# Seven instead of six feature tiles accumulated during the input's norm, with the tokens loaded first

## The chip, the cores and the metric

One Trainium2 chip, one core. The metric is the device time of one execution in microseconds; several executions are timed and their median is given. The engines are TensorE (PE), VectorE (DVE), ScalarE (ACT), GpSimdE (POOL) and SyncE (SP, whose queue issues nearly all DMAs).

## What is computed

One layer of a hybrid diffusion backbone in float32: 512 latent tokens (x) and 256 context tokens (ctx) of width 1024. Every token is normalised and modulated by scale and shift that come from a vector; one wide projection feeds a convolution module, a bidirectional mLSTM and two gates per channel; then come the output projection and an MLP. Cut to what matters here:

```python
sh1_l, sc1_l, ga1_l, sh2_l, sc2_l, ga2_l = silu(c) @ w_mod + b_mod      # split in six
sh1_c, sc1_c, *_ = silu(c_ctx) @ w_mod + b_mod
hl = rmsnorm(x, norm1_g) * (1 + sc1_l) + sh1_l
hc = rmsnorm(ctx, norm1_g) * (1 + sc1_c) + sh1_c
pl = split(hl @ w_in); pc = split(hc @ w_in)
y_conv = silu(layernorm(dwconv31(pl[0] * sigmoid(pl[1])))) @ w_conv_out
h_c, states = bi_mlstm(pc); h_l = bi_mlstm(pl, states)
y_m = (rmsnorm(h_l) * sigmoid(pl[5])) @ w_m_out
y = sigmoid(pl[7]) * y_conv + sigmoid(pl[8]) * y_m
x += ga1_l * (y @ w_out);  x += ga2_l * (relu(modulate(rmsnorm(x))@w1)**2 @ w2)
out = rmsnorm(x, final_g)
```

`pl[7]` and `pl[8]`, the gates per channel, are 16 feature tiles of 128 channels. They need nothing but `hl`, and the change is about where some of them are computed.

## The kernel before

**Products.** Every product is done in three passes on PE (`mm3`, L101): each operand is split into a rounded part (`hi`, a cast on ACT) and the rest (`lo`, a subtraction on DVE), and hi·hi, hi·lo and lo·hi are summed in PSUM. A weight tile is loaded by `wpiece` (L88): DMA into `wraw` (three buffers), cast `whi` on ACT (four buffers), `wlo` on DVE (four). The scheduler places every engine's instructions in one fixed order when the program is built; each engine then goes through its list in that order.

**The start.** SP issues `col` (all small constants), the row `c`, one tile of modulation weights `wm`, the four token tiles `xt2` to `xt5`, the second `wm`, and then the weights `was`. `crow` (L160) spreads the row over 128 partitions by a matmul with ones (`pcr`) and applies SiLU, which gives `cL` (and later `cC` from `c_ctx`). `xnorm` (L179) handles a token tile of 128x1024: square with sum on ACT (L181), the reciprocal root on POOL in two small steps (`rstd_`, L76 to L78), then the tile is scaled on DVE (L183). `moddot` (L195) gives scale and shift of 128 features, `m1`: two products with a sum on DVE (L199) and three operations on one column. `hmake` (L206) transposes 128 features of the four token tiles on PE into a PSUM bank `pt`, applies scale and shift on ACT (`hf`, two buffers, shared with `so` below), casts `hT` on ACT (L107) and takes its low part on DVE (L108).

**The first loop.** It runs over the eight slices j of 128 input features. Each round loads a slice of the gates' weights (`was[j]`, 128 x NS·128), makes `hT[j]`, and adds its product to NS accumulators `sacc`, one bank each, so that PE has work while the norm of the next slice is made. PSUM has eight banks, in two pools of four, "a" and "b". With NS = 6 the accumulators hold all of "a" and two of "b"; `pt`, `pcr`, `pg` (the convolution's projection), `ptc` (the context's transposes) and `pab` (gates' tiles computed later) all come from "b".

**Behind it.** The context tokens are normalised, `cC` is made, and each accumulator goes through a sigmoid (`so`) to DRAM (`sd`). Then the convolution's tiles (`pg`, `up`, and 31 taps `ca` on DVE), the gate tiles `ab_early` (NX = 3 here and NE = 3 later), the queries and keys, with the context's slices (`ctxpart`) in between, and the gates of the mLSTM (`p`, with `zm` as the result of `finish`).

Of the kernel before, what the change touches and what calls it, by code (L numbers as in the profile page):

```python
# [8 lines left out]
F32 = mybir.dt.float32  # L9
# [4 lines left out]
P = 128  # L14
# [7 lines left out]
HD = 512  # L22
FF = 4096
NFF = FF // P
NS = 6
NX = 3
NE = 3
NWM = 4
LOWP = 800 
# [18 lines left out]
def block(ctx, tc, a, out):  # L48
# [8 lines left out]


    col = cst.tile([P, NCOL], F32, name="col")
    nc.sync.dma_start(out=col, in_=a["col"])  # L60
    ident = cst.tile([P, P], F32, name="ident")
    make_identity(nc, ident)
    ones = cst.tile([P, P], F32, name="ones")
# [9 lines left out]
    def ccol(o, n=1):  # L73
        return col[:, o:o + n]
# [68 lines left out]
    with ExitStack() as hs:  # L143
# [16 lines left out]
        def crow(src, nm):  # L160
            r_ = p0.tile([P, D], F32, name=nm)
            nc.sync.dma_start(out=r_[0:1, :], in_=src)
            for n in range(2):
                nn = slice(n * 512, (n + 1) * 512)
                pc = bank("pcr")
                mm(pc, lhsT=ones[0:1, :], rhs=r_[0:1, nn], start=True, stop=True)
                nc.scalar.activation(out=r_[:, nn], in_=pc, func=AF.Silu)
            return r_
        cL = crow(a["c"][0:1, :], "cL")
        ssq = p0.tile([P, 6], F32, name="ssq")  # L170
        rs = p0.tile([P, 6], F32, name="rs")

        def xload(t):
            xt = p0.tile([P, D], F32, name=f"xt{t}")
            src = a["ctx"][t * P:(t + 1) * P, :] if t < 2 else a["x"][(t - 2) * P:(t - 1) * P, :]
            nc.sync.dma_start(out=xt, in_=src)
            return xt

        def xnorm(t, xt):  # L179
            junk = p0.tile([P, D], F32, tag="jnk", name="junk")  # L180
            nc.scalar.activation(out=junk, in_=xt, func=AF.Square, scale=1.0 / 32.0, accum_out=ssq[:, t:t + 1])  # L181
            rstd_(rs[:, t:t + 1], ssq[:, t:t + 1], 1)
            nc.vector.tensor_scalar(out=xt, in0=xt, scalar1=rs[:, t:t + 1], scalar2=None, op0=ALU.mult)  # L183

        m1 = p0.tile([P, 2, KT, 2], F32, name="m1")

        def modload(j, parts=(1, 0)):
            r = {}
            for s in parts:
                raw = p0.tile([P, D], F32, tag="wm", name="wm", bufs=NWM)  # L190
                nc.sync.dma_start(out=raw, in_=a["wmt"][s, j])
                r[s] = raw
            return r

        def moddot(j, c, cv, raws=None):  # L195
            raws = raws or modload(j)
            for s in (1, 0):
                raw = raws[s]
                nc.vector.scalar_tensor_tensor(out=raw, in0=raw, scalar=1.0, in1=cv, op0=ALU.mult, op1=ALU.mult,  # L199
                                               accum_out=m1[:, c, j, s:s + 1])  # L200
                nc.vector.tensor_scalar(out=m1[:, c, j, s:s + 1], in0=m1[:, c, j, s:s + 1],
                                        scalar1=ccol(O_BM + s * KT + j), scalar2=None, op0=ALU.add)
            nc.vector.tensor_scalar(out=m1[:, c, j, 1:2], in0=m1[:, c, j, 1:2], scalar1=1.0,
                                    scalar2=ccol(O_G1 + j), op0=ALU.add, op1=ALU.mult)

        def hmake(j, c, pt, tl, o):  # L206
            n = len(tl) * P
            for i, xt in enumerate(tl):
                nc.tensor.transpose(pt[:, i * P:(i + 1) * P], xt[:, j * P:(j + 1) * P], ident)
            hf = p0b.tile([P, T], F32, tag="hf", name="hf")  # L210
            nc.scalar.activation(out=hf[:, :n], in_=pt[:, :n], func=AF.Identity, scale=m1[:, c, j, 1:2],
                                 bias=m1[:, c, j, 0:1])
            split(hT[j][:, 0, o:o + n], hT[j][:, 1, o:o + n], hf[:, :n])

        raw0 = modload(0, (1,))
        xl = [xload(t + 2) for t in range(NT)]
        raw0 |= modload(0, (0,))
        for t in range(NT):
            xnorm(t + 2, xl[t])
        sacc = [(bank_a if i < 4 else bank)("sacc") for i in range(NS)]  # L220
        for j in range(KT):
            w = wpiece(a["was"][j], (NS, P))
            moddot(j, 0, cL, raw0 if j == 0 else None)
            hmake(j, 0, bank("pt"), xl, C)
            for i in range(NS):
                mm3(sacc[i], (w[0][:, i, :], w[1][:, i, :]), hsl(j, C, T), j == 0, j == KT - 1)
        xc = [xload(t) for t in range(2)]
        for t in range(2):
            xnorm(t, xc[t])
        cC = crow(a["cc"][0:1, :], "cC")  # L230
        for i in range(NS):
            so = p0b.tile([P, T], F32, tag="hf", name="so")
# [730 lines left out]
def build(shapes):  # L963
    import concourse.bacc as bacc
    import concourse.tile as tile

    nc = bacc.Bacc("TRN2", target_bir_lowering=False, num_devices=1)
    aps = {k: nc.dram_tensor(f"in_{k}", s, F32, kind="ExternalInput").ap() for k, s in shapes.items()}
    out = nc.dram_tensor("out_0_dram", (T, D), F32, kind="ExternalOutput").ap()
    with tile.TileContext(nc) as tc:  # L970
        block(tc, aps, out)
    return nc
# [10 lines left out]
```

## Time and profile before

| | |
|---|---|
| median of three timed runs | 1370.1 us (1367.97 to 1663.36) |
| the profiled execution | 1365.75 us, span 1364.0 us |
| PE, DVE, ACT, POOL busy | 97%, 70%, 44%, 4% of the span |
| mean granted TensorE clock | 0.993 |
| memory traffic over the span | 128 GB/s |

A row of the trace reads: start in us from the span's start, duration, engine, line, operation, output <- inputs, and in brackets how long the engine had stood idle and what ended that. Names are given without buffer numbers. A row "waited for" sums those idle times by the one that ended them.

### The profile page before, as it was taken

The page shows a single profiled execution, that of the slowest core. Times are in us where ns is not written, and L with a number is a line of the kernel's source. Part 1 is how long each engine was busy: PE and PEld are TensorE (multiplying, and loading weights), DVE is VectorE, ACT ScalarE, POOL GpSimd, SP SyncE. Part 2 cuts the span into 40 slices and gives each one's busy share as a digit, 9 for nine tenths or more (in the row PEclk, how much of TensorE's full clock was granted, in tenths as well). Part 3 has the DMA queues.
Part 4 walks back from the last instruction along what each step waited for, and adds up shares of the span by engine and source line. Part 5 has one row for each costly group of instructions (what it writes and reads, how often), then busy time and mean ns, then how long its engine had stood idle before and what let it go on. Part 6 is the DMA issues. An engine that isn't in the chain of part 4 may idle for free.

```text
span 1364.0 us, 16728 instructions
## 1 busy us (share of the span) xinstructions
PE 1327.2 (97%) x6264; PEld 1104.6 (81%) x6264; DVE 949.7 (70%) x1508; ACT 606.3 (44%) x931; POOL 55.3 (4%) x199
## 2 busy tenths in 40 slices
PE   5999899999999999999999999998999999999997
PEld 4788788888888888888888887787788888888886
DVE  6799988489674995849995464677676454545554
ACT  5547554446534465334645363222465322442232
POOL 1000100000000000000000000000010000000001
PEclk9999999999999999999999999999999999999999
DMA  8883233123322223221334465777623322333211
GB/s 316 291 318 99 87 97 120 62 67 97 108 93 63 77 88 120 79 76 64 108 93 145 153 232 185 253 260 225 204 77 115 102 78 77 123 109 94 69 54 62
DMA packets 64885, 175.30 MB, mean 129 GB/s; under 512 B 6546, under 2 KB 18978, under 8 KB 64804
## 3 DMA queue, kind: packets, MB, share of 16 engines
q1 hardware_dynamic: 64804, 174.23, 39.3%
q8 instruction: 49, 0.80, 0.2%
q14 instruction: 32, 0.26, 0.1%
HBM read 161.94 MB, written 12.26 MB: 128 GB/s over the span
## 4 chain that ended last, share of the span: by engine, by line
PE 79%; DMA 8%; DVE 6%; ACT 3%; issue 2%; POOL 1%; SPq 0%; ACTq 0%; POOLq 0%; DVEq 0%
PE pf L104 8%; PE pf L103 8%; PE pf L102 8%; PE pv L102 3%; PE pv L104 3%; PE pv L103 3%; DMA wraw<-in_wmo 2%; PE pl L102 2%; PE pg L104 2%; PE pg L102 2%; PE pl L103 2%; PE pq L104 2%; PE pq L102 2%; PE pq L103 2%; PE pl L104 2%
## 5 line engine op out<-in xcount | busy, mean ns | idle before, releaser
L97 ACT CAST whi<-wraw 128x1024 fp32r<-128x1024 f32 (+1 forms) x159 | 165.1, 1040 | 318.7 <-PE pv L104 74.6
L98 DVE TENSOR_TENSOR wlo<-wraw,whi 128x1024 fp32r<-128x1024 f32 (+1 forms) x159 | 191.6, 1207 | 97.7 <-ACT whi L97 96.9
L376 DVE SCALAR_TENSOR_TENSOR ca<-up,col,ca 128x512 f32<-128x512 f32 x240 | 179.6, 749 | 5.5 <-ACT ca L374 0.9
L336 DVE SCALAR_TENSOR_TENSOR cacc<-craw,col,cacc 128x512 f32<-128x512 f32 (+1 forms) x128 | 110.7, 880 | 0.1
L102 PE MATMUL pf<-w2h,fT 128*128 128x512 f32 x256 | 99.6, 389 | 0.0
L103 PE MATMUL pf<-w2l,fT 128*128 128x512 f32 x256 | 99.6, 389 | 0.0
L104 PE MATMUL pf<-w2h,fT 128*128 128x512 f32 x256 | 99.6, 389 | 0.0
L857 ACT CAST w2h<-w2raw 128x1024 fp32r<-128x1024 f32 x32 | 32.2, 1051 | 133.7 <-PE pf L104 107.1
L102 PE MATMUL pf<-h2T,whi 128*128 128x512 f32 x224 | 87.1, 389 | 0.0
L103 PE MATMUL pf<-h2T,whi 128*128 128x512 f32 x224 | 87.1, 389 | 0.0
L104 PE MATMUL pf<-h2T,wlo 128*128 128x512 f32 x224 | 87.1, 389 | 0.0
L877 DVE TENSOR_TENSOR x<-pf,x 128x512 f32<-128x512 f32 x64 | 44.1, 689 | 61.7 <-PE pf L104 61.7
L102 PE MATMUL pv<-whi,hT 128*128 128x512 f32 x192 | 75.4, 393 | 0.0
L104 PE MATMUL pv<-whi,hT 128*128 128x512 f32 x192 | 74.7, 389 | 0.0
L103 PE MATMUL pv<-wlo,hT 128*128 128x512 f32 x192 | 74.7, 389 | 0.0
L855 DVE TENSOR_TENSOR w2raw<-w2raw,ga 128x1024 f32<-128x1024 f32 x32 | 39.0, 1225 | 48.7 <-DMA w2raw<-in_w 47.7
L103 PEld LDWEIGHTS pf<-w2l,fT 128*128 128x128 f32 x256 | 48.1, 188 | 10.0
L102 PEld LDWEIGHTS pf<-w2h,fT 128*128 128x128 f32 x256 | 48.1, 188 | 10.0
L104 PEld LDWEIGHTS pf<-w2h,fT 128*128 128x128 f32 x256 | 48.1, 188 | 9.9
L103 PE MATMUL p<-wlo,hT 128*128 128x512 f32 x128 | 50.6, 395 | 2.4 <-DVE wlo L98 2.4
L102 PE MATMUL p<-whi,hT 128*128 128x512 f32 x128 | 50.8, 397 | 1.3 <-DVE zm L309 1.3
L645 DVE SCALAR_TENSOR_TENSOR wmt<-wmt,cB 128x1024 f32<-128x1024 f32 x32 | 39.1, 1223 | 17.5 <-DMA wmt<-in_wmt 15.6
(351 smaller groups left out, 3353.9 us busy)
## 6 DMA issues: line engine op xcount, KB each, us to landing
wm<-in_wmt SPq DMA_DIRECT2D x32, 512.0 KB, 5.7
wraw<-in_wqk SPq DMA_DIRECT2D x32, 512.0 KB, 3.5
wmt<-in_wmt SPq DMA_DIRECT2D x32, 512.0 KB, 3.8
wraw<-in_w SPq DMA_DIRECT2D x32, 512.0 KB, 3.6
w2raw<-in_w SPq DMA_DIRECT2D x32, 512.0 KB, 3.6
wraw<-in_wglu SPq DMA_DIRECT2D x16, 512.0 KB, 3.9
wraw<-in_wp SPq DMA_DIRECT2D x16, 512.0 KB, 3.6
wraw<-in_wv SPq DMA_DIRECT2D x16, 512.0 KB, 3.6
```

The source lines that it names most:

```text
L97: nc.scalar.copy(out=hi[:, s], in_=raw[:, s])
L98: nc.vector.tensor_tensor(out=lo[:, s], in0=raw[:, s], in1=hi[:, s].bitcast(F32), op=ALU.subtract)
L102: mm(dst, lhsT=l[0], rhs=r[0], start=start, stop=False)
L103: mm(dst, lhsT=l[0], rhs=r[1], start=False, stop=False)
L104: mm(dst, lhsT=l[1], rhs=r[0], start=False, stop=stop)
L336: nc.vector.scalar_tensor_tensor(out=acc[:, :n], in0=raw[:, d:d + n], scalar=ccol(wc + d), in1=acc[:, :n], op0=ALU.mult, op1=ALU.add)
L376: nc.vector.scalar_tensor_tensor(out=accv, in0=up[:, :, d:d + 64], scalar=w_, in1=accv, op0=ALU.mult, op1=ALU.add)
L645: nc.vector.scalar_tensor_tensor(out=raw, in0=raw, scalar=1.0, in1=cB, op0=ALU.mult, op1=ALU.mult, accum_out=modc[:, ch, j:j + 1])
L855: nc.vector.tensor_tensor(out=raw, in0=raw, in1=ga2, op=ALU.mult)
L857: nc.scalar.copy(out=hi, in_=raw)
L877: nc.vector.tensor_tensor(out=x1[t][:, nn], in0=pf, in1=x1[t][:, nn], op=ALU.add)
```

## The change

Seven accumulators instead of six (NS), two early gate tiles instead of three (NX), so the number of matmuls is unchanged and `was` pieces grow from 128x768 to 128x896. The four token tiles are loaded ahead of `col` and of both first `wm` tiles. The squares of the second and the fourth token tile are done on DVE with a sum, the others stay on ACT. The scale of a token tile is done in two pieces, columns 0 to 255 first and the other 768 behind the first `hmake`. `b1`, the modulation's offset plus one, is made once on POOL, so `moddot` has two small operations instead of three. The scratch for dynamic DMA is set to 4096.

```diff
-NS = 6
-NX = 3
+NS = 7
+NX = 2
@@
     col = cst.tile([P, NCOL], F32, name="col")
-    nc.sync.dma_start(out=col, in_=a["col"])
@@
-        def xnorm(t, xt):
-            junk = p0.tile([P, D], F32, tag="jnk", name="junk")
-            nc.scalar.activation(out=junk, in_=xt, func=AF.Square, scale=1.0 / 32.0, accum_out=ssq[:, t:t + 1])
+        cL = crow(a["c"][0:1, :], "cL")
+        xl = [xload(t + 2) for t in range(NT)]
+        nc.sync.dma_start(out=col, in_=a["col"])
...
+        def xstat(t, xt, dve=False):
+            junk = p0.tile([P, D], F32, tag=f"jnk{int(dve)}", name="junk")
+            if dve:
+                nc.vector.scalar_tensor_tensor(out=junk, in0=xt, scalar=1.0 / D, in1=xt, op0=ALU.mult, op1=ALU.mult,
+                                               accum_out=ssq[:, t:t + 1])
+            else:
+                nc.scalar.activation(out=junk, in_=xt, func=AF.Square, scale=1.0 / 32.0, accum_out=ssq[:, t:t + 1])
             rstd_(rs[:, t:t + 1], ssq[:, t:t + 1], 1)
-            nc.vector.tensor_scalar(out=xt, in0=xt, scalar1=rs[:, t:t + 1], scalar2=None, op0=ALU.mult)
+
+        def xscale(t, xt, o, n):
+            nc.vector.tensor_scalar(out=xt[:, o:n], in0=xt[:, o:n], scalar1=rs[:, t:t + 1], scalar2=None, op0=ALU.mult)
@@ moddot
-                nc.vector.tensor_scalar(out=m1[:, c, j, s:s + 1], in0=m1[:, c, j, s:s + 1],
-                                        scalar1=ccol(O_BM + s * KT + j), scalar2=None, op0=ALU.add)
-            nc.vector.tensor_scalar(out=m1[:, c, j, 1:2], in0=m1[:, c, j, 1:2], scalar1=1.0,
+            nc.vector.tensor_scalar(out=m1[:, c, j, 1:2], in0=m1[:, c, j, 1:2], scalar1=b1[:, j:j + 1],
                                     scalar2=ccol(O_G1 + j), op0=ALU.add, op1=ALU.mult)
+            nc.vector.tensor_scalar(out=m1[:, c, j, 0:1], in0=m1[:, c, j, 0:1], scalar1=ccol(O_BM + j),
+                                    scalar2=None, op0=ALU.add)
@@
-        raw0 = modload(0, (1,))
-        xl = [xload(t + 2) for t in range(NT)]
-        raw0 |= modload(0, (0,))
+        raw0 = modload(0)
         for t in range(NT):
-            xnorm(t + 2, xl[t])
+            xstat(t + 2, xl[t], t % 2 == 1)
+        nc.gpsimd.tensor_scalar(out=b1, in0=ccol(O_BM + KT, KT), scalar1=1.0, scalar2=None, op0=ALU.add)
+        for t in range(NT):
+            xscale(t + 2, xl[t], 0, 2 * P)
@@ first loop, behind hmake
+            if j == 0:
+                for t in range(NT):
+                    xscale(t + 2, xl[t], 2 * P, D)
@@ context
-            xnorm(t, xc[t])
+            xstat(t, xc[t])
+            xscale(t, xc[t], 0, D)
@@
-    nc = bacc.Bacc("TRN2", target_bir_lowering=False, num_devices=1)
+    nc = bacc.Bacc("TRN2", target_bir_lowering=False, num_devices=1, dynamic_dma_scratch_size=4096)
```

Three places show what this does to the engines' orders. The first is DVE's order from the program's start up to the modulation of the first slice, `m1`. Before:

```order
L199 SCALAR_TENSOR_TENSOR wm_124,m1_123<-wm_124,cL_113 128x1024
L201 TENSOR_SCALAR m1_123<-m1_123,col_66 128x1
L183 TENSOR_SCALAR xt2_126<-xt2_126,rs_122 128x1024
L203 TENSOR_SCALAR m1_123<-m1_123,col_66 128x1
L183 TENSOR_SCALAR xt3_128<-xt3_128,rs_122 128x1024
L183 TENSOR_SCALAR xt4_130<-xt4_130,rs_122 128x1024
L199 SCALAR_TENSOR_TENSOR wm_134,m1_123<-wm_134,cL_113 128x1024
L183 TENSOR_SCALAR xt5_132<-xt5_132,rs_122 128x1024
L201 TENSOR_SCALAR m1_123<-m1_123,col_66 128x1
```

And now:

```order
L182 SCALAR_TENSOR_TENSOR junk_141,ssq_129<-xt3_122 128x1024
L189 TENSOR_SCALAR xt3_122<-xt3_122,rs_130 128x256
L189 TENSOR_SCALAR xt2_120<-xt2_120,rs_130 128x256
L189 TENSOR_SCALAR xt2_120<-xt2_120,rs_130 128x768
L189 TENSOR_SCALAR xt3_122<-xt3_122,rs_130 128x768
L189 TENSOR_SCALAR xt4_124<-xt4_124,rs_130 128x256
L182 SCALAR_TENSOR_TENSOR junk_149,ssq_129<-xt5_126 128x1024
L189 TENSOR_SCALAR xt4_124<-xt4_124,rs_130 128x768
L189 TENSOR_SCALAR xt5_126<-xt5_126,rs_130 128x256
L189 TENSOR_SCALAR xt5_126<-xt5_126,rs_130 128x768
L206 SCALAR_TENSOR_TENSOR wm_133,m1_131<-wm_133,cL_112 128x1024
L208 TENSOR_SCALAR m1_131<-m1_131,b1_132,col_66 128x1
```

Both `wm` products were spread among the scales; now they stand behind all of them (the second `wm` follows on the last row shown), and the scales of the later columns stand ahead of them too.

The second place is PE's order behind the first round's accumulation, where the next slices are transposed. `pt_215` and `pt_257` are the banks of slices 1 and 2, `pt_299` that of slice 3; a row with "waits" waits for a semaphore of that engine. Before:

```order
L104 MATMUL sacc_161<-hT0_82,wlo_164 128x512
L209 MATMUL pt_215<-ident_68,xt2_126 128x128
...
L209 MATMUL pt_257<-ident_68,xt2_126 128x128 [waits PE_49]
...
L209 MATMUL pt_299<-ident_68,xt2_126 128x128 [waits Activation_49]
...
L102 MATMUL sacc_156<-hT1_83,whi_201 128x512 [waits Activation_49]
L102 MATMUL sacc_157<-hT1_83,whi_201 128x512
```

And now, with `pt_223` and `pt_267` for slices 1 and 2:

```order
L103 MATMUL sacc_164<-hT0_81,wlo_167 128x512
L216 MATMUL pt_223<-ident_67,xt2_120 128x128 [waits PE_49]
...
L216 MATMUL pt_267<-ident_67,xt2_120 128x128 [waits Activation_49]
...
L101 MATMUL sacc_158<-hT1_82,whi_210 128x512 [waits Activation_49]
L101 MATMUL sacc_159<-hT1_82,whi_210 128x512
```

Three slices stood together and the third waited for ACT's `hf` of the first; now two stand together and the second waits for it. Slices 3 and 4, and 5 and 6, are paired in the same way, and slice 7 is alone. In ACT's order the square of the second context token now stands between `hf` and the cast of `hT` of slice 5, and DVE's scale of that token ahead of that slice's low part; before, both squares stood behind the cast of slice 6.

The third place is ACT's order at the end of the first loop. `cC` is the context's row in two halves, `so` the sigmoid of an accumulator, `sacc_158` to `sacc_164` being the seven accumulators. Before:

```order
L167 ACTIVATE cC_508<-pcr_510 128x512 [waits DMAHW0_49,PE_49]
L167 ACTIVATE cC_508<-pcr_513 128x512 [waits PE_49]
L233 ACT_TABLE_LOAD
L233 ACTIVATE so_516<-sacc_156 128x512 [waits PE_49]
L233 ACTIVATE so_519<-sacc_157 128x512 [waits DVE_49,PE_49]
L97 CAST whi_589<-wraw_588 128x1024 [waits DMAHW4_49]
```

And now:

```order
L166 ACTIVATE cC_531<-pcr_533 128x512 [waits DMAHW0_49,PE_49]
L245 ACT_TABLE_LOAD [waits DVE_49]
L245 ACTIVATE so_539<-sacc_158 128x512 [waits PE_49]
L245 ACTIVATE so_542<-sacc_159 128x512 [waits DVE_49,PE_49]
L96 CAST whi_742<-wraw_741 128x1024 [waits DMAHW0_49,PE_49]
L166 ACT_TABLE_LOAD
L166 ACTIVATE cC_531<-pcr_536 128x512 [waits PE_49]
L245 ACT_TABLE_LOAD [waits DMAHW3_49]
L245 ACTIVATE so_545<-sacc_160 128x512 [waits Activation_49]
L245 ACTIVATE so_548<-sacc_161 128x512 [waits DMAHW4_49,Activation_49]
L96 CAST whi_793<-wraw_792 128x1024 [waits DMAHW1_49,PE_49]
L245 ACTIVATE so_551<-sacc_162 128x512 [waits DMAHW7_49,Activation_49]
```

The halves of `cC` stood together; now two sigmoids, a cast and a table load stand between them. The cast `whi_742` takes the buffer of the loop's last `was` piece. On PE the first `pg` uses the bank of the second half's `pcr`, `ptc` the bank of `sacc_162`, and the second `pg` that of `sacc_163`. In DVE's order four products of the context's modulation stood ahead of the first product for the convolution, `up`; now eight do.

More of the change, by code (lines that the diff above doesn't have):

```diff
@@ L168, in crow @@
             return r_
-        cL = crow(a["c"][0:1, :], "cL")
-        ssq = p0.tile([P, 6], F32, name="ssq")
-        rs = p0.tile([P, 6], F32, name="rs")
         def xload(t):
@@ L177, in xload @@
             return xt
-        def xnorm(t, xt):
-            junk = p0.tile([P, D], F32, tag="jnk", name="junk")
-            nc.scalar.activation(out=junk, in_=xt, func=AF.Square, scale=1.0 / 32.0, accum_out=ssq[:, t:t + 1])
+        cL = crow(a["c"][0:1, :], "cL")
+        xl = [xload(t + 2) for t in range(NT)]
+        nc.sync.dma_start(out=col, in_=a["col"])
+        ssq = p0.tile([P, 6], F32, name="ssq")
+        rs = p0.tile([P, 6], F32, name="rs")
+        def xstat(t, xt, dve=False):
[5 more added lines that the diff above has]
+                nc.scalar.activation(out=junk, in_=xt, func=AF.Square, scale=1.0 / 32.0, accum_out=ssq[:, t:t + 1])
             rstd_(rs[:, t:t + 1], ssq[:, t:t + 1], 1)
-            nc.vector.tensor_scalar(out=xt, in0=xt, scalar1=rs[:, t:t + 1], scalar2=None, op0=ALU.mult)
+        def xscale(t, xt, o, n):
+            nc.vector.tensor_scalar(out=xt[:, o:n], in0=xt[:, o:n], scalar1=rs[:, t:t + 1], scalar2=None, op0=ALU.mult)
         m1 = p0.tile([P, 2, KT, 2], F32, name="m1")
+        b1 = p0.tile([P, KT], F32, name="b1")
         def modload(j, parts=(1, 0)):
```

## The prediction

> **What bounds the kernel now.** I read the page's first part, then the chain of work that ended last, then what TensorE (PE) waits for, then the first 165 us by windows.
>
> ```profile
> span 1364.0 us, 16728 instructions
> PE 1327.2 (97%) x6264; PEld 1104.6 (81%) x6264; DVE 949.7 (70%) x1508; ACT 606.3 (44%) x931; POOL 55.3 (4%) x199
> PE 79%; DMA 8%; DVE 6%; ACT 3%; issue 2%; POOL 1%; SPq 0%; ACTq 0%; POOLq 0%; DVEq 0%
> ```
>
> PE is busy for all but 37 of 1364 us. The change leaves the count of large matmuls alone, so all it can move is those 37 us and their like: the start and PE's waits in the part of the program it touches.
>
> ```profile
> engine line waited for: us in total, times, longest us
> PE pt L209 <- DVE xt L183: 7.9, 4, 4.0
> PE pcr L166 <- DMA cL<-in_c: 3.2, 1, 3.2
> PE sacc L102 <- ACT hT L107: 2.4, 2, 2.1
> PE p L103 <- DVE wlo L98: 2.4, 1, 2.4
> PE p L102 <- DVE zm L309: 1.3, 1, 1.3
> PE pt L209 <- ACT hf L211: 0.9, 2, 0.4
> ```
>
> The list of PE's waits shows 13.2 us of waiting before the first `sacc` matmul (7.9 + 3.2 + 2.1), then almost nothing in the eight rounds of the first loop (0.9 for `hf`, 0.3 for `hT`), then 2.4 and 1.3 at the gate projection's successor `p`.
>
> ```profile
> core 0: us, PE busy (x) PEld busy (x) DVE busy (x) ACT busy (x) POOL busy (x), PEclk, DMA share, GB/s
> 20.00:62.00 42.00, 40.80 (x182) 31.83 (x181) 35.59 (x75) 21.29 (x31) 3.11 (x4) 1.00 0.79 282
> 80.00:100.00 20.00, 20.00 (x92) 16.47 (x91) 19.96 (x40) 8.73 (x14) 0.00 (x0) 1.00 0.88 318
> 100.00:150.00 50.00, 50.00 (x280) 43.68 (x280) 48.51 (x61) 31.85 (x43) 2.01 (x12) 1.00 0.24 72
> 150.00:165.00 15.00, 11.25 (x46) 8.37 (x45) 14.93 (x18) 7.78 (x13) 0.32 (x6) 0.89 0.45 139
> ```
>
> By windows, the first loop (20 to 62 us) already keeps PE busy for 40.8 of 42. From 80 to 165 us VectorE (DVE) is full as well, and PE loses to it only at the end (11.25 of 15). The dependence orders of both programs coincide again behind the gates, so a shift that is there at 230 us stays to the end.
>
> **The change part by part. The start.** The rows of the start, by the chain and the timeline:
>
> ```profile
> 3.36 8.55 DMA xt<-in_x
> 7.02 0.60 ACT L167 ACTIVATE cL<-pcr 128x512 f32<-128x512 f32 x1 [1.11 <-PE pcr L166]
> 8.09 1.06 ACT L181 ACTIVATE junk<-xt 128x1024 f32<-128x1024 f32 x1 [0.48 <-DMA xt<-in_x]
> 9.34 0.19 POOL L77 TENSOR_SCALAR rs<-ssq 128x1 f32<-128x1 f32 x1 [7.18 <-ACT junk L181]
> 9.61 0.56 POOL L78 TENSOR_TENSOR rs<-rs,nhalf 128x1 f32<-128x1 f32 x1
> 10.20 0.75 DVE L183 TENSOR_SCALAR xt<-xt,rs 128x1024 f32<-128x1024 f32 x1 [1.07 <-POOL rs L78]
> 10.87 0.21 DVE L203 TENSOR_SCALAR m<-m,col 128x1 f32<-128x1 f32 x1
> 13.82 1.22 DVE L199 SCALAR_TENSOR_TENSOR wm<-wm,cL 128x1024 f32<-128x1024 f32 x1
> 14.96 0.08 DVE L199 DVE_READ_ACCUMULATOR wm<-wm,cL 128x1 f32 x1
> 14.04 1.41 POOL L78 TENSOR_TENSOR rs<-rs,nhalf 128x1 f32<-128x1 f32 x1
> 16.80 0.78 ACT L211 ACTIVATE hf<-pt,m 128x512 f32<-128x512 f32 x1 [1.76 <-PE pt L209]
> 17.48 0.82 ACT L97 CAST whi<-wraw 128x768 fp32r<-128x768 f32 x1
> 18.20 0.62 ACT L107 CAST hT<-hf 128x512 fp32r<-128x512 f32 x1
> 18.87 2.50 PE L102 MATMUL sacc<-hT,whi 128*128 128x512 f32 x5 [2.11 <-ACT hT L107]
> ```
>
> The last token lands at 11.9 (3.36 + 8.55). The first is there at about 8.05, so three further 512 KB took 3.85 us, 1.28 each. `col` (252 KB) and one `wm` tile no longer stand ahead, 1.5 such loads: the tokens land from about 6.1 to 10.0, 1.9 us earlier. ACT can't use that for its first square: the SiLU of `cL` ends at 7.62 in any case. ACT's two squares (1.25 each, from 8.09 to where POOL starts at 9.34) then end at about 8.9 and 10.2. DVE's squares have no row; the nearest is L199, the same operation and shape, 1.14 to its accumulator's read and 1.22 in all. POOL adds 0.83 (from 9.34 to 10.17). A scale of 1024 columns steps 0.67 (10.20 to 10.87) and one of one column about 0.13, so 256 columns are estimated at 0.27 and 768 at 0.54.
>
> DVE's order of the change, replayed: square of the second token 7.4 to 8.6; its first columns and the first token's, behind POOL, to about 10.0 or 10.3; four more scales, the fourth token's square, and its two scales behind POOL's 0.83 to 14.1 or 15.2. Only then come both `wm` products, 2 x 1.22 and the two small operations, 2.55: `m1` is ready at 16.7 to 17.8. Before, one product ran at 7.65 and the other inside the scales' wait, so `hf` started at 16.80. The half-microsecond between the ends is POOL: a POOL step beside a DVE product took 1.41 instead of 0.56 (14.04, beside 13.82 to 14.96). I take 17.3, since the fourth token's statistics run beside a scale. With 896 instead of 768 columns in the weight cast that stands between `hf` and `hT`, 0.1 more: first `sacc` at 19.6 for 18.87, **+0.7** (bounds -0.1 and +1.5). Loading tokens first thus buys nothing, as the products go to the back.
>
> [...] If both new squares each cost a POOL step 0.85 more the head would stand at +1.6 or so; by the replay POOL has no work beside either, and the sum goes without it.
>
> **The first loop.** Seven accumulators take four "a" and three "b" banks; one "b" bank is left for `pt` where two were. In PE's new order the transposes of rounds 1 and 2, 3 and 4, 5 and 6 stand in pairs, and the second of a pair waits until ACT's `hf` has emptied the first. PE idles for `hf` (0.78), then for what ACT does up to the `hT` cast, less the second transposes' 0.45:
>
> ```profile
> 53.48 0.60 PE L209 MATMUL pt<-ident,xt 128*128 128x128 f32 x4
> 54.01 2.06 PE L166 MATMUL pcr<-cC,ones 1*128 1x512 f32 x4
> 56.40 1.66 PE L102 MATMUL sacc<-hT,whi 128*128 128x512 f32 x6 [0.33 <-ACT hT L107]
> 60.63 0.39 PE L102 MATMUL pg<-hT,whi 128*128 128x512 f32 x1
> 54.80 1.03 ACT L97 CAST whi<-wraw 128x1024 fp32r<-128x1024 f32 x1
> 57.35 1.28 ACT L233 ACT_TABLE_LOAD   x1
> 58.65 1.09 ACT L233 ACTIVATE so<-sacc 128x512 f32<-128x512 f32 x2
> 70.93 0.56 ACT L211 ACTIVATE hf<-ptc,m 128x256 f32<-128x256 f32 x1 [3.57 <-DMA sd<-so]
> ```
>
> Pair (1,2) has a weight cast of about 0.9 and the `hT` cast of 0.6 in between: 0.78 + 1.05 = 1.8. Pair (3,4): 0.78 + 0.15 = 0.9. Pair (5,6) has the square of a context token there (1.25) and the scale of it on DVE ahead of `hT`'s low part: 0.78 + 1.4 = 2.2. Round 7 took 2.4 before (54.0 to 56.40, with both `pcr` pieces inside); now one `pcr` waits for `hf`: 2.1. With the 0.9 that before lost to `hf` taken off, the loop costs 1.8 + 0.9 + 2.2 - 0.3 - 0.9 = **+3.7** (bounds 0, if ACT is early each time, and +5).
>
> **The end of the loop.** Before, `pg` followed `sacc` at once (60.63). Now its bank is that of the second `pcr`, which ACT empties only after a weight cast that waits for the loop's last-but-one matmul, and a table load: 1.03 + 1.28 + 0.6 = 2.9, less 0.7 that PE still has to do, and 0.3 of `pcr` that moved here: **+2.5**. The `ptc` transposes behind `pg` wait for a sigmoid `so`, queued behind a cast that waits for `pg`'s last-but-one matmul: 1.03 + 0.55 - 0.23 = 1.4, and the next `pg` for one more `so`, +0.3: **+1.7**. Queued behind those two `so` are the context's `hf` and, by its store (70.93 waited 3.57 for one), DVE's next steps. Together the end costs +4.2 (bounds +1, if the casts are early, and +6).
>
> **From there to the gates.** DVE's saturated stretch ran from its first `up` at 72.3 to the `wlo` that PE lacked at 157.03, 84.7 us. By the order four products of 1.15 with their small operations now come before `up`, one weight's low part (1.2) and some small operations are gone: about 77.4 are left. `up` comes at about 88 (PE's shift, the extra tile of 24 x 0.2277 = 5.46, and the store's wait): 165.4, where PE would be there at 154.6 + 8.6 = 163.2. So the wait stays at about 2, and the DVE work saved is spent on the later start. The wait for `zm` (1.3) may go, as its copy stands 1.6 us earlier in DVE's order: half of it, **-0.7**.
>
> ```profile
> 157.03 0.51 PE L103 MATMUL p<-wlo,hT 128*128 128x512 f32 x1 [2.42 <-DVE wlo L98]
> 158.33 0.63 PE L102 MATMUL p<-whi,hT 128*128 128x512 f32 x1
> 158.76 0.63 PE L103 MATMUL p<-wlo,hT 128*128 128x512 f32 x1
> ```
>
> **The clock.** After the wait of 2.42, matmuls step 0.43 instead of 0.23 (158.33 to 158.76) for 3 us, 1.4 lost. Two of the new idles are of that size (2.2 each), so I add one such dip: **+1.4** (bounds 0 and three, +4.2). [...]
>
> The larger DMA scratch moves nothing that has a row: nearly all packets are of another queue kind. The seventh tile adds 64 KB to each round's 1.4 MB, and the round lasts 0.68 longer, so the load of 282 GB/s doesn't rise.
>
> **Sum:** 0.7 + 3.7 + 4.2 - 0.7 + 1.4 = +9.3 on the profiled execution's 1365.75: 1375. That execution lies 4.35 below the median of the timed runs and 2.2 below their fastest; the same +9.3 on the median is 1379. I predict 1377, between them.
>
> **The rivals.** *DVE catches up (0 to +5).* If `up` starts at 86 and not at 88, DVE reaches the first `p` at 163.4, when PE does; 2.4, the other half of `zm`'s 1.3 and the dip of 1.4 go, and +9.3 becomes about +4.8. For it: DVE has 7 us less there; against: the store's wait ahead of `up`. *The start pays (faster, -2 to -7).* The waits for `hf` are hidden, because ACT is far ahead and the dependence that I counted as PE's idle falls beside PE's backlog; tokens 1.9 earlier make the first `sacc` earlier by that much if POOL and DVE keep up with the landings; and DVE's relief removes the 3.7 and 1.4 of the `p` stage: -1.9 - 5.1 = -7 at most. It decides from the point where `m1` is ready before 16.3 and the pairs cost under 1 us each. Against it stand the two products at the back of DVE's order and the single bank. *The clock falls after every new idle (slower, +14 to +28).* Six idles of 1 to 2.2 us, each with 1.4, and a second round of waits on ACT from slower matmuls: +9.3 + 7 = +16, and more only if DVE's stretch grows too. *The order as executed is not what I replayed*, and nothing happens: within 2 of before.
>
> **How the numbers follow.** The forecast, +5 to +14, has 0.58; DVE catching up 0.15; no effect 0.08; the start paying 0.14; the clock 0.05. From the middle of the timed and the profiled run, 1367.9, the range of eight in ten takes in -4 and +18: 1364 to 1386. A measurement of this kernel tells 2% (27 us) from no change; only the clock's far end reaches that on the slow side, and nothing on the fast side but an error of mine: 0.02 faster, 0.95 within, 0.03 slower.
>
> **What would show it.** First `sacc` between 18.8 and 20.4; `pt` waiting for `hf` three times or four, 0.7 to 0.8 each; `sacc` waiting for `hT` 0.2 to 1.4 behind each pair; `pg` waiting for `cC` about 2, `ptc` and the next `pg` for `so` 1.7 in all; `p` waiting for `wlo` 2 or so. A first `sacc` before 18, or no wait for `hf` in the loop, would make the prediction wrong on the fast side; slow clock after each pair on the other.

## The result, and the profile after

Four runs of the changed kernel took 1382.51 to 1385.19 us, median 1384.11, against 1369.57 before: the ratio is 1.0105 [1.0093, 1.0117], a loss of 14.5 us. That is inside the forecast range (1364 to 1386) and within the 2% called no change; the predicted 1377 was 7 too low. The profiled execution took 1385.19. It is the slowest of the four, while before's 1365.75 lies under all but one of the 70 further runs of that kernel taken with the experiments (1365.29 to 1373.52, median 1369.6). The two profiles, 19.4 apart, therefore show more than the change costs. A second profile of the same kernel, below, tells which of the differences stay.

The same three lines of the page as before:

```profile
span 1383.4 us, 16729 instructions
PE 1335.1 (97%) x6264; PEld 1107.4 (80%) x6264; DVE 952.3 (69%) x1499; ACT 607.2 (44%) x929; POOL 52.1 (4%) x200
PE 77%; DMA 8%; DVE 8%; ACT 4%; issue 2%; POOL 1%; SPq 0%; POOLq 0%; ACTq 0%; DVEq 0%
```

The matmuls are as many as before, but PE is busy 7.9 us longer and idle 11.5 us longer (48.3 for 36.8). So there are two losses: waits, and matmuls that run slower. The list of PE's waits in the changed kernel gives the first (an excerpt; line numbers are those of the changed kernel):

```profile
PE sacc L101 <- ACT hT L106: 6.7, 3, 5.1
PE pt L216 <- DVE xt L189: 6.6, 3, 3.5
PE pwo L101 <- DVE sig L739: 6.0, 1, 6.0
PE pt L216 <- ACT hf L218: 2.6, 3, 0.9
PE pg L101 <- ACT cC L166: 1.8, 1, 1.8
PE p L102 <- DVE wlo L97: 1.8, 1, 1.8
PE ptc L216 <- ACT so L245: 1.4, 1, 1.4
PE p L101 <- DVE zm L321: 1.3, 1, 1.3
```

The rows for `hf`, `cC` and `so` are new or larger. The timeline says where each lies; in brackets is how long PE had stood idle and what ended that:

```profile
19.36 1.22 PE L101 MATMUL sacc<-hT,whi 128*128 128x512 f32 x2 [5.11 <-ACT hT L106]
28.26 0.66 PE L216 MATMUL pt<-ident,xt 128*128 128x128 f32 x4 [0.87 <-ACT hf L218]
29.60 1.65 PE L101 MATMUL sacc<-hT,whi 128*128 128x512 f32 x6 [0.69 <-ACT hT L106]
40.73 0.66 PE L216 MATMUL pt<-ident,xt 128*128 128x128 f32 x4 [0.87 <-ACT hf L218]
52.52 0.66 PE L216 MATMUL pt<-ident,xt 128*128 128x128 f32 x4 [0.87 <-ACT hf L218]
54.06 1.65 PE L101 MATMUL sacc<-hT,whi 128*128 128x512 f32 x5 [0.88 <-ACT hT L106]
67.10 1.12 PE L165 MATMUL pcr<-cC,ones 1*128 1x512 f32 x2 [0.87 <-ACT hf L218]
77.66 0.50 PE L101 MATMUL pg<-hT,whi 128*128 128x512 f32 x1 [1.77 <-ACT cC L166]
86.43 0.44 PE L216 MATMUL ptc<-ident,xt 128*128 128x128 f32 x2 [1.41 <-ACT so L245]
```

Three pairs of transposes stop for 0.87 each while ACT empties the only bank; the `hT` casts behind two of the pairs add 0.69 and 0.88; then come the `pcr` piece (0.87), `pg` (1.77) and `ptc` (1.41). Together 8.2, where before lost 1.2 in the same place.

The slower matmuls are in three stretches. In the windows, the columns after the length are busy time of PE, PEld, DVE, ACT and POOL; then PEclk, the granted clock:

```profile
55.40:58.81 3.41, 3.27 (x9) 2.36 (x9) 2.15 (x3) 0.89 (x1) 0.00 (x0) 0.54 0.55 195
69.05:72.46 3.41, 3.41 (x10) 2.62 (x9) 0.85 (x1) 2.46 (x4) 0.00 (x0) 0.54 0.46 101
79.30:82.71 3.41, 3.41 (x10) 2.70 (x9) 3.41 (x9) 0.70 (x2) 0.00 (x0) 0.55 0.81 219
```

In each, PE is busy nearly throughout, does 9 or 10 matmuls in place of 15 (they step 0.43 instead of 0.23), and loses about 1.7 us. Before had none of these in its first 100 us.

### The profile page after: what moved, and what is told of

The parts are those of the page before. It is cut to its first block, busy times and chain, and to the rows that moved or that the text cites. A ratio compares the mean times of both kernels' runs of the same rounds, so it can differ in the third digit from the quotient of the medians.

```text
span 1383.4 us, 16729 instructions
## 1 busy us (share of the span) xinstructions
PE 1335.1 (97%) x6264; PEld 1107.4 (80%) x6264; DVE 952.3 (69%) x1499; ACT 607.2 (44%) x929; POOL 52.1 (4%) x200
## 4 chain that ended last, share of the span: by engine, by line
PE 77%; DMA 8%; DVE 8%; ACT 4%; issue 2%; POOL 1%; SPq 0%; POOLq 0%; ACTq 0%; DVEq 0%
PE pf L102 8%; PE pf L103 8%; PE pf L101 8%; PE pv L103 3%; PE pv L101 3%; PE pv L102 3%; DVE wlo L97 3%; PE pg L101 2%; PE pg L103 2%; PE pg L102 2%; PE pl L102 2%; PE pl L101 2%; PE pl L103 2%; DMA wraw<-in_wmo 2%; DMA wraw<-in_wco 2%
## 5 line engine op out<-in xcount | busy, mean ns | idle before, releaser
L101 PE MATMUL pg<-hT,whi 128*128 128x512 f32 x128 | 51.5, 402 | 1.8 <-ACT cC L166 1.8
```

The source lines that it names most:

```text
L101: mm(dst, lhsT=l[0], rhs=r[0], start=start, stop=False)
```

## The experiments

Each kernel was timed in turn with the kernel before on the same chip, and its ratio is to those runs. The theory under test: the loss comes from the eighth bank, which the seventh accumulator takes, and the rest of the change is neutral.

**Everything but the seventh accumulator** (edit to the changed kernel):

```diff
-NS = 7
-NX = 2
+NS = 6
+NX = 3
```

> The changed kernel with six accumulators and three early gate tiles, as before the change; everything else of the change stays. Theory (the seventh accumulator takes the second bank of pt): the slices are transposed three at a time again, the waits for hf in the first loop fall from 2.6 to about 0.9 us in all, the slow-clock stretches behind them go, and only the start (+0.5) and the split making of cC stay: 1369 to 1375 us, 10 to 14 below the changed kernel. Rival (the new start and the new orders cost the time): at least 1379 us, and half-clock stretches in the loop stay.

Measured: 1369.28 (1367.12 to 1370.18), ratio 0.9995 [0.9986, 1.0005]. PE's waits for `hf` are back to their old size, and those on `cC` and `so` are gone from the list:

```profile
PE sacc L101 <- ACT hT L106: 5.6, 2, 5.0
PE p L102 <- DVE wlo L97: 2.5, 1, 2.5
PE pt L216 <- ACT hf L218: 0.9, 2, 0.4
```

Tokens first, two squares on DVE and split scales, together, are worth nothing measurable beside six accumulators.

**The seventh accumulator alone** (edit to the kernel before):

```diff
-NS = 6
-NX = 3
+NS = 7
+NX = 2
```

> The kernel before with seven accumulators and two early gate tiles, nothing else of the change. Theory: three waits of 0.8 to 0.9 us for hf, stretches at half clock behind some of them, pg or ptc waiting at the loop's end, 1378 to 1384 us. Rival (the start and the orders of the rest cost the time): within 3 us of before, 1367 to 1372.

Measured: 1379.31 (1379.09 to 1382.94), ratio 1.0077 [1.0057, 1.0097]. All three new waits are there, without any other part of the change:

```profile
PE pt L209 <- ACT hf L211: 2.6, 3, 0.9
PE ptc L209 <- ACT so L233: 2.0, 1, 2.0
PE pg L102 <- ACT cC L167: 1.8, 1, 1.8
```

With the first experiment this settles which part makes the loss: this one alone costs 9.3 us in these runs, and the rest alone nothing. The whole change lost 11.6 and 14.5 in its two timings; the interval here overlaps both of theirs, so it isn't shown that the parts together cost more than this one. No run gives the tile its accumulator without taking a bank: the step from the tile to the bank rests on the rows of the waits.

**The context's row `cC` made at the start** (edit to the changed kernel), which takes `pcr` from the loop's end:

```diff
-        cL = crow(a["c"][0:1, :], "cL")
+        cL = rowload(a["c"][0:1, :], "cL")
+        cC = rowload(a["cc"][0:1, :], "cC")
+        crow(cL)
...
+        crow(cC)
...
-        cC = crow(a["cc"][0:1, :], "cC")
```

> The changed kernel with the row c_ctx loaded at the start and cC made there, before the first loop; seven accumulators stay. Theory (cC's second half, behind a cast and a table load, costs PE 1.8 us, two pcr pieces and a slow-clock stretch at the end of the loop): pg follows sacc at once, 4 to 6 us less than the changed kernel, 1378 to 1380 us. Rival (VectorE's full stretch up to p takes back what PE gains): p waits that much longer for wlo, 1382 to 1385 us.

Measured: 1378.48 (1374.7 to 1381.84), ratio 1.0064 [1.0038, 1.0089], 5.6 under the changed kernel's first timing and 2.8 under the second one below. The wait for `cC` went, but `pg` now waits 1.1 for `hf`, the first `sacc` moved from 19.36 to 21.61 because `cC`'s four `pcr` pieces (3.62) and SiLU stand ahead of a square on ACT, and the wait for `zm` grew from 1.3 to 2.9.

**`cC` made in the middle of the loop** (edit to the changed kernel):

```diff
+            if j == 2:
+                cC = crow(a["cc"][0:1, :], "cC")
...
-        cC = crow(a["cc"][0:1, :], "cC")
```

> The changed kernel (seven accumulators, its own start) with cC made in the middle of the first loop, behind its third round, and not at the end. Theory (the split cC costs at the loop's end): pg follows sacc at once, so 1.8 of waiting, one pcr and the slow-clock stretch behind them go, while two pcr and a wait of about 1 come in the fourth round: 1378 to 1381 us, first sacc at 19.4 as in the changed kernel. Rival (VectorE's full stretch up to p sets the time): p waits for wlo or zm that much longer, 1383 to 1386 us.

Measured: 1378.02 (1377.08 to 1380.74), ratio 1.007 [1.0057, 1.0083]. The waits near it show the exchange:

```profile
39.85 1.12 PE L165 MATMUL pcr<-cC,ones 1*128 1x512 f32 x2 [0.69 <-ACT cC L166]
41.66 0.66 PE L216 MATMUL pt<-ident,xt 128*128 128x128 f32 x4 [0.69 <-ACT cC L166]
43.19 0.89 PE L216 MATMUL pt<-ident,xt 128*128 128x128 f32 x4 [0.87 <-ACT hf L218]
...
69.99 0.50 PE L101 MATMUL pg<-hT,whi 128*128 128x512 f32 x1 [1.14 <-ACT hf L218]
...
81.90 0.44 PE L216 MATMUL ptc<-ident,xt 128*128 128x128 f32 x2 [1.41 <-ACT up L369]
```

The wait for `cC` ahead of `pg` is gone. In its place stand two of 0.69 for `cC`'s pieces in the loop and 1.14 for `hf`, as `pg` now takes its turn on the bank behind `pt`. (A few of its matmuls moved ahead of the last `sacc` ones, so the place to compare is `ptc`: 81.90 instead of 86.43, and instead of 84.06 in the second profile below.) The median is 6.1 under the changed kernel's first timing and 3.2 under the second, whose ratio interval overlaps this one, so a gain is not clearly shown. With one bank, `cC` costs PE time in each of the three places tried.

**Idle time filled** (edit to the changed kernel): four matmuls with zero weights into `sacc` behind the transposes of slices 1, 3, 5 and 7, so that PE has work while ACT empties the bank. They add nothing to the sums.

```diff
+        zr = p0.tile([P, P], F32R, name="zr")
...
+            if j % 2:
+                for i in range(4):
+                    mm(sacc[i], lhsT=zr, rhs=hT[0][:, 0, C:C + T], start=False, stop=False)
```

> The changed kernel with four products of a zero weight tile added into accumulators behind the transposes of slices 1, 3, 5 and 7 (they add nothing to the result, 4 x 0.23 us of PE each), where PE idles 0.87 for hf. Theory (idle of 1.7 to 2.3 in a few microseconds sets off the half clock): the waits for hf shrink to 0.1, the half-clock stretches at 56 and 69 us go or shrink, 1380 to 1382.5 us, although PE has 3.6 us more work. Rival (the stretches come at their time whatever PE does in those waits): both stretches stay, 1384 to 1386 us.

Measured: 1382.73 (1380.58 to 1385.36), ratio 1.0102 [1.0088, 1.0117]. The waits of `pt` for `hf` are gone from the list (`sacc` still waits 6.7 for `hT`), and the slow stretches at 55 and 69 too, yet the time lies between the changed kernel's two timings. The filling takes the place of the waits. For the question whether the waits lower the clock, it is inconclusive, as the next run shows.

**The changed kernel again**, unaltered:

> The changed kernel once more, unaltered, with a profile of its own, to see which of its half-clock windows are its own. Theory (which windows fall to half clock depends on how the idles lie to windows of 3.4 us, so it differs between executions): not the same three windows of the first 100 us at half clock in this profile, 1379 to 1384 us. Rival (the squares on VectorE and the stretches belong to the kernel): the same three, 1383 to 1385 us, and the kernel with all squares on ScalarE really is 5 us faster.

Measured: 1381.26 (1378.91 to 1386.56), ratio 1.0089 [1.007, 1.0107], 11.6 over the kernel before in the same runs. Its profile is one of the faster executions (1379.48, span 1377.7). The new waits are the same to 0.01, but for one of 0.36 that came in at 56.38. The windows differ:

```profile
52.79:56.20 3.41, 2.09 (x9) 1.28 (x9) 1.23 (x2) 3.38 (x7) 0.74 (x2) 1.00 1.04 417
56.20:59.61 3.41, 3.23 (x14) 2.70 (x15) 1.88 (x3) 0.62 (x1) 0.00 (x0) 1.00 0.52 168
76.68:80.09 3.41, 3.41 (x10) 2.63 (x9) 3.41 (x7) 0.96 (x2) 0.00 (x0) 0.50 0.87 213
```

Two of the three slow stretches aren't there: the granted clock is 1.00 from 25.5 to 76.68. The third is, 2.3 earlier, behind `pcr` and `pg`. So the waits belong to the kernel, and how many of them are followed by half a clock belongs to the execution. The mean clock says the same: 0.990 over 1383.4 is 6.9 us more lost to the clock than 0.995 over 1377.7, and the two spans differ by 5.7. Before shows it too: its runs at 0.995 took 1365.3 to 1368.9, those at 0.991 1369.5 to 1373.5.

The traces also show what went ahead of the slow stretches. In the profiles of before and after the granted clock changes only at the borders of stretches of 3.41 us that follow one another without a gap, and where these borders fall differs: the first clock record begins at 21.70 before and at 24.38 after. Cut along them, from that record to 7 us before the end, the two traces hold 776 stretches at full clock, nine of which were followed by half a clock. In those nine PE was busy with other work than the `pcr` pieces, whose weights have one row, for 1.13 to 1.70 us. Three more had 1.65, 1.65 and 2.07 and were followed by full clock, as were the other 764, which had 2.10 or more. The first row below is of the first profile, ahead of its slow stretch at 55, the others of the first experiment's kernel, with six accumulators:

```profile
51.69:55.10 3.41, 1.70 (x9) 1.28 (x9) 1.07 (x2) 3.38 (x6) 0.74 (x2) 1.00 1.01 406
```

```profile
59.46:62.88 3.42, 3.42 (x11) 1.67 (x11) 1.23 (x1) 2.21 (x4) 0.00 (x0) 1.00 0.98 316
62.88:66.29 3.41, 3.41 (x9) 2.63 (x9) 2.90 (x7) 3.38 (x5) 0.00 (x0) 0.50 0.63 256
```

In the first profile both idles of the pair (5,6) lie in one stretch, which leaves PE 1.70 of work, and the next runs at half a clock; in the second the borders lie otherwise, 2.09 is left, and the clock stays. With six accumulators PE did not stop at all ahead of a slow stretch, but 1.98 of the 3.42 are four `pcr` pieces; before's four, 1.82 in the stretch from 52.42, were followed by full clock. In the two executions of the changed kernel an idle thus counted by what it left of the stretch it fell in.

**All squares on ACT** (edit to the changed kernel), since two of them on DVE hold up the products there:

```diff
-            xstat(t + 2, xl[t], t % 2 == 1)
+            xstat(t + 2, xl[t])
```

> The changed kernel with all four squares of the tokens on ScalarE; seven accumulators and everything else of the change stay. Theory (VectorE's squares and their POOL round trips delay the wm products that stand behind all scales): the last scale ends at about 13.2 instead of 14.2, m1 at 15.8, first sacc at 18.0 to 18.5 instead of 19.4, 1382 to 1384 us. Rival (the squares on VectorE help): first sacc after 19.4, 1384 to 1387 us.

Measured: 1378.99 (1378.49 to 1379.53), ratio 1.0065 [1.0051, 1.0078]. The first `sacc` came at 18.88, 0.5 earlier; the waits of the loop are the same, with one slow stretch (at 76). Against the run above, 1381.26 with runs from 1378.91 on, no difference that is more than the clock's share is shown.

**Both edits: squares on ACT and `cC` in mid-loop**:

```diff
-            xstat(t + 2, xl[t], t % 2 == 1)
+            xstat(t + 2, xl[t])
...
+            if j == 2:
+                cC = crow(a["cc"][0:1, :], "cC")
...
-        cC = crow(a["cc"][0:1, :], "cC")
```

> The changed kernel with seven accumulators, all four squares on ScalarE and cC made in the middle of the loop. Theory (three causes that add up: the bank's waits, cC at the loop's end, the start): 1373 to 1377 us, with pt still waiting 2.6 us for hf, so still above before. Rival (each of the two edits only moved the half-clock windows): 1377 to 1380 us, no better than either alone.

Measured: 1379.01 (1378.57 to 1379.15), ratio 1.0068 [1.0049, 1.0086]. The two don't add up: `ptc` stands at 83.30, later than with `cC` in mid-loop alone, behind two slow stretches between 40 and 48, and `p` waits 3.0 for `zm` as it did there.

The other four ask whether the start can be made to pay with six accumulators.

**Start and `cC` rearranged** (`cC` early, one `wm` ahead of the tokens, `col` last, two squares on DVE):

```diff
-NS = 7
-NX = 2
+NS = 6
+NX = 3
...
-        raw0 = modload(0)
+        raw0 = modload(0, (1,))
+        xl = [xload(t + 2) for t in range(NT)]
+        raw0 |= modload(0, (0,))
+        nc.sync.dma_start(out=col, in_=a["col"])
...
+        crow(cC)
...
-        cC = crow(a["cc"][0:1, :], "cC")
```

> Six accumulators, cC made at the start, and one wm tile loaded ahead of the tokens and the other right behind them, with col last; the rest of the change's start (two squares on VectorE, scales in two pieces, two small operations) stays. Both wm products then stand among the scales and not behind them. Theory (the products' place at the back made the earlier tokens worthless): first sacc at 16.5 to 17.5 us, no wait for hf over 0.5, pg right behind sacc; 1361 to 1367 us, faster than before by 3 to 8. Rival (VectorE's full stretch decides when p starts): the gain turns into a longer wait of p for wlo, 1367 to 1371 us.

Measured: 1373.6 (1372.22 to 1376.24), ratio 1.0028 [1.0018, 1.0038]: slower than before, where 1361 to 1367 was expected. The first `sacc` came at 22.8 (16.5 to 17.5 expected). The timeline of ACT and DVE shows a chain through three engines:

```profile
9.43 0.60 ACT L169 ACTIVATE cC<-pcr 128x512 f32<-128x512 f32 x1 [1.11 <-PE pcr L168]
9.92 1.05 ACT L188 ACTIVATE junk<-xt 128x1024 f32<-128x1024 f32 x1
...
12.29 1.22 DVE L185 SCALAR_TENSOR_TENSOR junk<-xt 128x1024 f32<-128x1024 f32 x1
14.77 0.88 DVE L192 TENSOR_SCALAR xt<-xt,rs 128x256 f32<-128x256 f32 x2 [0.72 <-POOL rs L77]
19.11 1.22 DVE L209 SCALAR_TENSOR_TENSOR wm<-wm,cL 128x1024 f32<-128x1024 f32 x1
```

`cC` held ACT until 9.92, so the first square came 3.4 later than in the changed kernel (6.51); then squares on DVE, roots on POOL and scales on DVE followed one another, and the last product began at 19.11.

**The same start without `cC`, all squares on ACT**:

```diff
+        raw0 = modload(0, (1,))
+        xl = [xload(t + 2) for t in range(NT)]
+        raw0 |= modload(0, (0,))
+        nc.sync.dma_start(out=col, in_=a["col"])
...
-            xstat(t + 2, xl[t], t % 2 == 1)
+            xstat(t + 2, xl[t])
```

> Six accumulators; the first wm tile ahead of the tokens, the second behind them, col last; all four squares on ScalarE; scales in two pieces and two small operations as in the change. Theory (squares on VectorE form a chain with POOL and the products stood at the back): first sacc at 16.2 to 17.2 us, 2 earlier than before, 1366 to 1368 us. Rival (a wait behind it, pg for cC or p for wlo, takes the gain back): 1369 to 1371 us.

Measured: 1368.81 (1364.5 to 1371.44), ratio 0.9998 [0.9988, 1.0007], though the first `sacc` came at 16.89, 2.0 earlier than before. Where the 2.0 went, by windows of this kernel and then of before, from the first `up` of before to its wait at `p`:

```profile
72.00:157.00 85.00, 83.11 (x429) 69.93 (x428) 82.56 (x117) 47.41 (x69) 2.01 (x12) 1.00 0.45 157
```

```profile
72.00:157.00 85.00, 82.61 (x431) 70.09 (x429) 82.63 (x121) 47.64 (x69) 2.01 (x12) 1.00 0.44 155
```

DVE is busy for all but 2.4 of 85 in both. The first `pg` was 1.5 earlier than before (59.1 for 60.6), the second 0.65 (65.55 for 66.2), the first `pv` 0.1 (214.4 for 214.5). So the loop kept 1.5 of the 2.0, the loop's end took 0.9 and DVE's stretch the rest: PE arrives early at an engine that is full.

**With `cC` in the middle of that loop**:

```diff
+            if j == 4:
+                cC = crow(a["cc"][0:1, :], "cC")
...
-        cC = crow(a["cc"][0:1, :], "cC")
```

> As the kernel with six accumulators, the first wm tile ahead of the tokens and all squares on ScalarE, and cC made behind the fifth round, so that no table load stands between the halves. Theory: first sacc at 16.2 to 17.2, pg right behind sacc, 1363 to 1366.5 us, faster than before by 0.3 to 0.5%. Rival (p waits for VectorE's wlo whatever PE gains ahead of it): p waits 4 to 6 us there, 1368 to 1371 us.

Measured: 1370.34 (1368.15 to 1375.24), ratio 1.0014 [1.0002, 1.0026]. `p` waits 4.0 for `wlo`: the earlier PE is, the longer it waits there, as the rival had it.

**With the context's small operations on POOL**, to relieve DVE:

```diff
+            eng = nc.gpsimd if c else nc.vector
...
-            nc.vector.tensor_scalar(out=m1[:, c, j, 1:2], in0=m1[:, c, j, 1:2], scalar1=b1[:, j:j + 1],
+            eng.tensor_scalar(out=m1[:, c, j, 1:2], in0=m1[:, c, j, 1:2], scalar1=b1[:, j:j + 1],
...
```

> The kernel with six accumulators, the first wm tile ahead of the tokens and all squares on ScalarE, with the two small operations of each of the context's eight modulation slices moved from VectorE to POOL (16 x 0.13 us of VectorE's full stretch between 72 and 157 us). Theory (that stretch takes back what the start gains): p's waits for wlo and zm, 1.3 and 1.4 in that kernel, shrink to under 1 in sum and its slow-clock stretch goes; 1364 to 1367 us. Rival (p is not held by VectorE's sum of work, or POOL's steps make the context's hf late): p waits as before, 1368 to 1371 us.

Measured: 1369.86 (1364.5 to 1374.18), ratio 1.0 [0.9986, 1.0013]. The price on POOL is in the window from 70 to 100 and in the timeline:

```profile
70.00:100.00 30.00, 30.00 (x139) 24.57 (x138) 27.72 (x44) 13.51 (x23) 11.49 (x10) 1.00 0.90 325
```

```profile
83.14 2.09 POOL L207 TENSOR_SCALAR m<-m,b,col 128x1 f32<-128x1 f32 x1 [4.35 <-DVE wm L204]
```

Ten operations on one column took 11.49 us, 1.15 each; on DVE they step 0.13 to 0.2. `p` still waited 3.4 for `wlo`.

## Why the prediction was right, and where it was off

The program's landmarks (first matmul of each) split the two profiles of the changed kernel against before's. What the seventh tile adds, 5.46, is taken off:

| step | predicted | first profile | second profile |
|---|---|---|---|
| first `sacc` | +0.7 | +0.5 | +0.6 |
| waits from there to the second `pg` | +7.9 | +7.0 | +7.4 |
| the clock in the same stretch | +1.4 | +6.2 | +3.2 |
| rest of that stretch | 0 | +1.5 | +1.7 |
| second `pg` to first `pv` | -0.7 | -0.6 | -0.8 |
| behind it | 0 | +4.8 | +1.7 |
| span | +9.3 | +19.4 | +13.7 |

The second `pg` stood at 66.2 before, at 86.92 and 84.54 after; the first `pv` at 214.5, 229.1 and 226.5.

**The head** was right in its reason, and in its size with some luck. Both `wm` products stood behind all scales and `hf` waited for the second:

```profile
6.02 0.60 ACT L166 ACTIVATE cL<-pcr 128x512 f32<-128x512 f32 x1 [1.11 <-PE pcr L165]
6.51 1.05 ACT L185 ACTIVATE junk<-xt 128x1024 f32<-128x1024 f32 x1
14.16 1.22 DVE L206 SCALAR_TENSOR_TENSOR wm<-wm,cL 128x1024 f32<-128x1024 f32 x1
15.62 1.22 DVE L206 SCALAR_TENSOR_TENSOR wm<-wm,cL 128x1024 f32<-128x1024 f32 x1
17.18 0.78 ACT L218 ACTIVATE hf<-pt,m 128x512 f32<-128x512 f32 x1 [3.29 <-DVE m L210]
```

One step in it failed: `cL`'s SiLU was to end at 7.62 "in any case", and it ended at 6.62, since the row `c` no longer waits behind `col` (PE's wait for `pcr` ended at 3.2, now at 2.2). It changed little, because `m1` was late at DVE: the scales ended at the early bound, about 14.2, but the products and their small operations, put at 2.55 (its terms give 2.7), took 2.9, from 14.16 to 17.09. So `m1` came near the 17.3 that was taken. The square of 1.14 to 1.22 on DVE was right (1.22, stepping 1.15).

**The waits** were right in place and, within 0.9, in sum. Single ones were off: the pair (1,2) cost 0.87 + 0.69 for 1.8, (3,4) 0.87 for 0.9, (5,6) 0.87 + 0.88 for 2.2 (and 0.36 more in the second profile), round 7 took about 1.9 from the end of its transposes to `sacc`, 0.87 of it idle, for 2.1, `pg` waited 1.77 for 2.2, `ptc` 1.41 for 1.4, and the 0.3 of the next `pg` did not come. The mechanism at `pg`, a weight cast that waits for the loop's matmuls and a table load in front of `cC`, is in ACT's rows:

```profile
74.65 1.04 ACT L96 CAST whi<-wraw 128x1024 fp32r<-128x1024 f32 x1 [3.12 <-PE sacc L102]
75.72 1.28 ACT L166 ACT_TABLE_LOAD   x1
77.01 0.60 ACT L166 ACTIVATE cC<-pcr 128x512 f32<-128x512 f32 x1
```

**The clock** is the term furthest off in the profiles. One dip of 1.4 was added. The second profile has one stretch of 1.7, and its slow matmuls of the start last until 25.4, 5.9 from the first `sacc`, where before it was 3.0: at half speed that is 1.5 more. The first has three stretches, 5.1, and 1.1 from the start. The upper bound of the term, 4.2 for three dips, thus stood 2 below what the first profile lost. Much of both figures is chance, though. The start's part is not the seventh accumulator's: with six, the steps of 0.43 lasted for 2.7 from the first `sacc` before (18.87 to 21.59) and for 5.9 in the first experiment's kernel (19.30 to 25.24). And over all timed runs the granted clock averages 0.9931 in the 70 of before and 0.9919 in the ten of the changed kernel, which makes 9.4 and 11.2 us lost: 1.7 more (estimated from clocks of three digits, give or take 0.8), near the 1.4 that was added. What the sum left out was rather the rest of that stretch, below. The rival that the clock falls after each new idle (+14 to +28) is not what happened, as eight idles brought one stretch in one execution and three in the other, but it points to the right term: the first timing's +14.5 lies where it begins, the second's +11.6 within the forecast (+5 to +14).

**From there to the gates** the sum came out right by luck. DVE's stretch from the first `up` (92.69) to the `wlo` that PE lacked (172.91) took 80.2, where before it took 84.7 and 77.4 were forecast; PE's wait fell from 2.4 to 1.8. The wait for `zm` stayed at 1.3, so the half of it that was taken off did not go. PE's idle time up to `pv` is 5.1 before and 5.3 and 5.1 after, so in sum no wait went. In its place before's slow stretch at 158.3 went, which was not in the sum.

**Behind `pv`** nothing was forecast, and 1.7 to 4.8 came. The two differ by the clock: PE is busy there for 1132.2 before, 1133.7 in the first and 1131.1 in the second profile, as between 1000 and 1030 before has one slow stretch, the first two and the second none. PE's idle time there grew by 3.3 and 2.8. The larger part is the wait of `pwo` for `sig`, 4.1 in before's profile, 6.0 and 6.6 in these; but 5.1 and 6.4 also in the profiles of the two kernels with six accumulators that were as fast as before. So that wait is before's low profile and not the change. The sum was made against that profile; the 9.3 put on the median of before gives 1379, which is 2 under the changed kernel's second timing and 5 under its first.

The rival "DVE catches up" fell, as `p` still waited; so did "the start pays", on both of its conditions: `m1` was not ready before 16.3 (`hf` started at 17.18), and the pairs (1,2) and (5,6) cost over 1 us. The rest of 1.5 to 1.7 between the first `sacc` and the second `pg` is in no row of waits; an estimate from the matmuls' steps in the second profile finds about 1.3 of it where PE stops. The last transpose ahead of a wait takes 0.27 us where one in the stream steps 0.11, so each stop costs the overlap with the next matmul too. What stays open: what else the rest holds, and why half a clock followed the stretch from 51.69 of the first profile, with 1.70 us of work, and not the one from 171.15, with 1.65.

## What to carry to other kernels

Before one more accumulator is given a bank, list who takes turns on the banks that are left: with one bank, each eviction that stood beside PE's work becomes a wait, 0.87 here for one of 0.78, and everything queued ahead of it on the evicting engine (a weight cast, a table load) adds to it. Each such stop also cost overlap (0.27 for a last transpose that steps 0.11 in the stream), and 1.7 more where half a clock followed, as behind one idle of 0.87 beside 1.12 of one-row matmuls. An earlier start is worth only what the next full engine can use: 2.0 us at the first accumulation were 0.1 us at 215, behind a stretch in which DVE has 2.4 us free in 85. Judge a gain of a few microseconds by several executions, and take a profile's own time into account, since the runs of the kernel before lie 8 us apart.

## What the runs showed of the hardware

- Half a clock came in stretches of 3.41 us, one or two in a row (two from 953.5 before and from 969.9 after), and cost 1.7 each where PE was busy. In the first 100 us of after such stretches followed idles of 0.87 and 0.88, an idle of 0.87 beside 1.12 of one-row matmuls, and an idle of 1.77; in the first experiment's kernel one followed four one-row matmuls (1.98) without any idle. Two executions of the changed kernel, with the same waits but for one of 0.36, had three and one of them within the first 100 us.
- At the start, matmuls step 0.43 us although the granted clock reads 1.00 there, as a window and two matmuls of the changed kernel show: the step is the surer sign. This trace holds no clock record before 24.4 us, and the window counts that time as full clock.

```profile
22.00:26.00 4.00, 4.00 (x14) 3.20 (x13) 4.00 (x8) 0.00 (x0) 0.00 (x0) 1.00 0.81 240
```

```profile
22.44 0.63 PE L101 MATMUL sacc<-hT,whi 128*128 128x512 f32 x1
22.87 0.63 PE L102 MATMUL sacc<-hT,whi 128*128 128x512 f32 x1
```

- An operation of one column on POOL took 1.15 us on average while DVE was busy for 27.7 of 30 us. One by one, the fourteen between 61 and 98 us of that kernel took 0.28 to 0.30 five times and 0.99 to 2.30 nine times. In before one took 1.41 beside a DVE product (at 14.04), the three of the same line ahead of it 0.55 or 0.56. What makes them longer is not shown.
